# Turning the second layer's softmax weights on VectorE and through DRAM instead of on TensorE

## The chip, the cores and the metric

The kernel runs on one core of one Trainium2 chip. The metric is the device time of one execution in microseconds (us), taken as the median of several runs. Five engines matter here, each with its own queue that it works off strictly in order: TensorE (PE: matmuls, with its weight loads shown as PEld), VectorE (DVE), ScalarE (ACT), GpSimd (POOL, all but idle in this kernel) and SyncE (SP), which issues nearly all the transfers (DMAs). [...]

## The reference

Two decoder layers on a sequence of T = 512 tokens of width D = 2048, all in float32. The first layer is differential attention, the second "forgetting" attention over one shared set of keys and values. The change touches the second layer only. Cut to it, the reference is:

```
k, v, F = shared_kv(...)                       # F[t, head]: running sum of log forget gates
q, g = split(h @ w_q)                          # 16 heads of 128
for each block of 128 queries t, each head:
    sc = q[t] . k[s] / sqrt(128) + F[t] - F[s],   -1e30 where s > t
    p  = softmax(sc over s)
    o  = sum over s of p[t, s] * v[s]
y = (o * silu(g)) @ w_out
x = layer_norm(alpha * x + gate * y)
```

## The kernel before

**Products.** Every float32 operand X of a matmul is split into a rounded part hi (type fp32r) and the rest lo = X - hi. A product A x B is then three matmuls, hi x hi, hi x lo and lo x hi (`products`, lines 174 to 176). ScalarE makes hi (a copy that rounds), VectorE makes lo (a subtraction).

**The weight stream.** Weights come in "subs" of 256 rows by up to 512 columns: SP loads them (`wst`, four buffers), ScalarE copies them to `whi` (line 94), VectorE subtracts to `wlo` (line 95); `whi` and `wlo` have three buffers each. A `group` is one block of 512 output columns: 8 subs, and for each sub four "bursts" of six 512-wide matmuls, one burst for each PSUM bank (`acc`). So a group has 32 bursts and 192 `acc` matmuls. After its last burst each bank is read out (`evac`): for the second layer two banks become q (hi and lo) of two heads, two become their SiLU gates.

**Pieces between bursts.** After each burst `tick` takes one entry from a list, `pieces`, and runs it. In the second layer the pieces of a group are the attention of the pair of heads (a and b) whose q the group before made. So attention of pair p - 1 is laid into the matmuls of group p (`bj[p]`, eight groups), and the last pair into the first group of the output projection (`oB`), which starts right after.

**Attention of one head** (`attention_b`). A query block i of 128 has w = 128 (i + 1) keys. `score(i)`: three matmuls into `sc`, `biasb` from F and the mask (line 1208), sum and row minimum of the negated scores in one DVE instruction (line 1214), exponential with row sum on ScalarE (line 1217), reciprocal and scaling on VectorE (lines 1218, 1219). The result `eb` has queries on the partitions, but `values` needs keys on the partitions. `turn(i)` does that: i + 1 TensorE transposes of 128x128 into the PSUM tile `tr` (line 1228), ScalarE copies `tr` to `pTh` (line 1231), VectorE subtracts to `pTl` (line 1232). `values` then does twelve matmuls into `o` with `pTh` and `pTl` as moving operands, and line 1246 multiplies by the gate (`ogB`). There is one `pTh` and one `pTl`, so head b may write them only when head a's `values` have read them.

`attention_pair` fixes at which burst each step is handed over. The instructions are not run in that order: the framework plans every engine's queue anew from its own estimate of when each input is ready, and keeps that order on the chip. A few DVE instructions (line 1305, the first scaling of the residual, `nr`) are kept in the order in which they were written.

**The end of the layer.** In the first group of `oB` the last head's output must pass `ogB`, then `split_ogb` (`hh` on ScalarE, `hl` on VectorE), before the last k-tile of that same group can be multiplied. The same group also scales four residual tiles `nr` by two DVE instructions each (lines 1305 and 1306). `residual_b` puts these into entries of `pieces` that are None, from the third on, and the rest at the end of the list. When the group ends, line 926 (`ztmp`) empties each `acc` bank, and the next group waits for that.

Of the kernel before, what the change touches and what calls it, by code (L numbers as in the profile page):

```python
# [10 lines left out]
F32 = mybir.dt.float32  # L11
F32R = mybir.dt.float32r
I32 = mybir.dt.int32
AF = mybir.ActivationFunctionType
ALU = mybir.AluOpType

P = 128
D = 2048
KT = D // P
T = 512  # L20
TB = T // P
# [89 lines left out]
def tile_yoco(  # L111
# [23 lines left out]
    nc = tc.nc  # L135
    V, S, PE, G = nc.vector, nc.scalar, nc.tensor, nc.gpsimd
# [11 lines left out]
    dram = ctx.enter_context(tc.tile_pool(name="dram", bufs=1, space=bass.MemoryType.DRAM))  # L148
# [13 lines left out]
    def tr_bank(name="tr"):  # L162
        return ps.tile([P, 512], F32, name=name, tag="tr", bufs=1)
# [8 lines left out]
    def products(dst, lhs, rhs, start, stop):  # L172

        PE.matmul(dst, lhs[0], rhs[0], start=start, stop=False)  # L174
        PE.matmul(dst, lhs[0], rhs[1], start=False, stop=False)  # L175
        PE.matmul(dst, lhs[1], rhs[0], start=False, stop=stop)  # L176


    ident = const.tile([P, P], F32, name="ident")
# [3 lines left out]
    mask = const.tile([P, 512], F32, name="mask")  # L183
# [16 lines left out]
    pt = tr_bank()  # L200
# [7 lines left out]
    pt = tr_bank()  # L208
# [200 lines left out]
    def mod_rows(pool, fours, dst, bias, one):  # L409

        red = []

        def steps(n, acc):
            if n == 0:
                red.append(pool.tile([P, 64], F32, name="mred", tag="mred", bufs=2))
            t = pool.tile([P, 512], F32, name="mturn", tag="mturn", bufs=1)
            V.transpose(t, acc)
            V.tensor_reduce(  # L420
                red[0][:, 16 * n : 16 * n + 16], t.rearrange("p (j q) -> p j q", q=32), axis=mybir.AxisListType.X, op=ALU.add
            )
            if n == 3:
                row = pool.tile([64, 32], F32, name="mrow", tag="mrow", bufs=1)
                nc.sync.dma_start(row, bias.rearrange("(j q) -> j q", q=32))
            yield True
            if n == 3:
                pt = tr_bank()
                PE.matmul(pt[0:64, 0:32], red[0], fours, start=True, stop=True)
                V.scalar_tensor_tensor(row, pt[0:64, 0:32], one, row, op0=ALU.add, op1=ALU.add)  # L430
                nc.sync.dma_start(dst.rearrange("o (j q) -> (o j) q", q=32), row)
        return steps
# [5 lines left out]
    part = {}  # L438
    with tc.tile_pool(name="start", bufs=2, reuse_waits="tile") as sp, tc.manual_schedule(engines={ET.DVE}):
# [44 lines left out]
        def mod_steps():  # L484
            for n, (i, k, nr) in enumerate(tiles):
                k0, nk = sets[i]
                load_mods(n + NBUF)
                if k >= KT - on_pe(i):
                    continue
                if k == 0:  # L490
                    accs[i] = sp.tile([P, 2, 2 * P], F32, name="sacc", tag="sacc", bufs=2)
                acc = accs[i][:, :, : nk * P]
                for kq in range(nr):
                    w, sc = loaded[i, k][:, kq, :, :], cact[:, k + kq : k + kq + 1]
                    if k + kq == 0:
                        V.tensor_scalar(acc, w, sc, None, op0=ALU.mult)
                    else:
                        V.scalar_tensor_tensor(acc, w, sc, acc, op0=ALU.mult, op1=ALU.add)  # L498
                    yield i
# [3 lines left out]
        steps = mod_steps()  # L503
# [76 lines left out]
        todo = [(u, kt, kt == k0, kt == k1 - 1) for u, k0, k1 in phases for kt in range(k0, k1)]  # L580

        at = {"set": 0, "kt": 0, "go": 0}
        summed, turned = [], []
# [67 lines left out]
    for dst, src, col, bias, one in (  # L651
# [5 lines left out]
        steps = mod_rows(ap, fours, dst, bias[col : col + D], one)  # L657
# [358 lines left out]
    npool, n, nstats = zp  # L1016
# [83 lines left out]
    for i, (half, s) in enumerate(lag):  # L1100
# [7 lines left out]
        hi, lo = held[s]  # L1108
# [13 lines left out]
    for dst, col, one in ((mod_dram[1][1:2, :], D, 1.0), (gate_dram[1], 2 * D, 0.0)):  # L1122
        steps = mod_rows(npool, fours, dst, b_mod[1, col : col + D], one)
# [25 lines left out]

    bctx = ExitStack()  # L1150
    bp = bctx.enter_context(tc.tile_pool(name="bp", bufs=1, reuse_waits="tile"))
    pTh = bp.tile([P, TB, T], F32R, name="pTh")
    pTl = bp.tile([P, TB, T], F32R, name="pTl")

    V.tensor_scalar(pTh[:, 3, 256:384], mask[:, 0:P], 0.0, None, op0=ALU.mult)
    V.tensor_scalar(pTl[:, 3, 256:384], mask[:, 0:P], 0.0, None, op0=ALU.mult)
    ogB = [None] * B_HEADS

    def evac_b(p):
        def fn(b, acc):  # L1160
            hd = 2 * p + b % 2
            if b < 2:
                hi = bp.tile([P, T], F32R, name="qh", tag="qh", bufs=2)
                lo = bp.tile([P, T], F32R, name="ql", tag="ql", bufs=2)
                S.activation(hi, acc, AF.Copy, scale=QS)
                V.scalar_tensor_tensor(lo, acc, QS, hi.bitcast(F32), op0=ALU.mult, op1=ALU.subtract)
                cur[hd, "q"] = (hi, lo)
            else:
                th = bp.tile([P, T], F32, name="thb", tag="thb", bufs=1)
                sg = bp.tile([P, T], F32, name="sgb", tag="sgb", bufs=2)  # L1170
                S.activation(th, acc, AF.Tanh, scale=0.5)
                V.scalar_tensor_tensor(sg, th, 1.0, acc, op0=ALU.add, op1=ALU.mult)
                cur[hd, "sgT"] = sg
        return fn
# [21 lines left out]
    def attention_b(hd):  # L1196
        st = {}

        def score(i):
            def fn():  # L1200
                w = (i + 1) * P
                m = max(w, 256)
                q, k = cur[hd, "q"], cur[hd, "kB"]
                sc = sc_bank()
                ts = slice(i * P, (i + 1) * P)
                products(sc[:, :m], (q[0][:, ts], q[1][:, ts]), (k[0][:, :m], k[1][:, :m]), True, True)
                bias = bp.tile([P, 512], F32, name="biasb", tag="biasb", bufs=2)
                V.scalar_tensor_tensor(
                    bias[:, :w], cur[hd, "nf"][:, :w], F[:, i, hd : hd + 1], mask[:, (3 - i) * P :], op0=ALU.add, op1=ALU.add
                )  # L1210
                e = bp.tile([P, 512], F32, name="eb", tag="eb", bufs=3)
                mn = bp.tile([P, 1], F32, name="mnb", tag="mnb", bufs=3)
                rs = bp.tile([P, 1], F32, name="rsb", tag="rsb", bufs=3)
                V.tensor_tensor_reduce(  # L1214
                    out=e[:, :w], in0=sc[:, :w], in1=bias[:, :w], scale=-1.0, scalar=3.0e38, op0=ALU.add, op1=ALU.min, accum_out=mn
                )
                S.activation(e[:, :w], e[:, :w], AF.Exp, bias=mn, scale=-1.0, accum_out=rs)  # L1217
                V.reciprocal(rs, rs)
                V.tensor_scalar(e[:, :w], e[:, :w], rs, None, op0=ALU.mult)
                st["e", i] = e  # L1220
            return fn

        def turn(i):
            def fn():
                pt = tr_bank()
                e = st["e", i]
                for j in range(i + 1):
                    PE.transpose(pt[:, j * P : (j + 1) * P], e[:, j * P : (j + 1) * P], ident)  # L1228
                ts = slice(i * P, (i + 1) * P)
                src = pt[:, : (i + 1) * P].rearrange("p (j t) -> p j t", t=P)  # L1230
                S.copy(pTh[:, 0 : i + 1, ts], src)  # L1231
                V.tensor_tensor(pTl[:, 0 : i + 1, ts], src, pTh[:, 0 : i + 1, ts].bitcast(F32), op=ALU.subtract)  # L1232
            return fn

        def values(j0, j1):
            def fn():
                if j0 == 0:
                    st["o"] = o_bank()
                vh, vl = cur[hd // 2, "vB"]
                es = slice((hd % 2) * P, (hd % 2 + 1) * P)  # L1240
                for j in range(j0, j1):
                    t0 = min(j * P, 256)
                    products(st["o"][:, t0:], (vh[:, j, es], vl[:, j, es]), (pTh[:, j, t0:], pTl[:, j, t0:]), j == 0, j == 3)
                if j1 == TB:
                    ogB[hd] = ktile("ogB")
                    V.scalar_tensor_tensor(ogB[hd], st["o"], 0.5, cur[hd, "sgT"], op0=ALU.mult, op1=ALU.mult)
            return fn

        return [score(i) for i in range(TB)], [turn(i) for i in range(TB)], [values(0, 2), values(2, 4)]

    def attention_pair(p):
        sa, ta, va = attention_b(2 * p)
        sb, tb, vb = attention_b(2 * p + 1)
        return [
            None, None, sa[0], sa[1], ta[0], sa[2], ta[1], sa[3], ta[2], sb[0], ta[3], sb[1], va[0], sb[2], va[1], None, tb[0],
            tb[1], sb[3], tb[2], None, tb[3], None, vb[0], vb[1],
        ]

    def split_ogb(hds):
        for hd in hds:  # L1260
# [115 lines left out]
```

## Time and profile before

| | us |
|---|---|
| median of 3 runs (1995.78 to 1996.25) | 1996.07 |
| the profiled execution | 1992.9 |
| its span in the trace | 1991.1 |
| TensorE busy | 1955.8 (98%) |
| VectorE busy | 1320.8 (66%) |
| ScalarE busy | 708.2 (36%) |

The span runs from the first to the last instruction in the trace; the profiled execution has 1.8 us around it. Names in the profile are the program's tile names, `out<-in`; L1228 is line 1228 of the kernel. `DMA_DIRECT2D` is a transfer being issued by SP; "to landing" is the time from its issue until its data are there. The second layer's groups with attention lie from about 1420 us to 1850 us of the span, 54 us each.

### The profile page before, as it was taken

What the parts mean: (1) busy time and instruction counts of PE and PEld (TensorE: products, weight loads), DVE (VectorE), ACT (ScalarE), POOL (GpSimd) and SP (SyncE); (2) the same over time, 40 slices, a digit from 0 to 9 for tenths busy, and PEclk for the clock granted to TensorE, in tenths of its full rate; (3) what the DMA queues carried; (4) which work ended last, traced back from release to release, by engine and by line L of the source; (5) the groups of instructions that cost most, each with busy time, mean ns of one, the idle gap of its engine ahead of it and who ended that gap; (6) DMA issues with size and microseconds to landing.
All of it is one profiled execution on the core that took longest, in us unless ns stands there. A gap on an engine that the chain in (4) does not pass through costs nothing.

```text
span 1991.1 us, 24748 instructions
## 1 busy us (share of the span) xinstructions
PE 1955.8 (98%) x9079; PEld 1618.8 (81%) x9079; DVE 1320.8 (66%) x2404; ACT 708.2 (36%) x1217; POOL 2.2 (0%) x10
## 2 busy tenths in 40 slices
PE   5999999999999999999999999999999999999997
PEld 4888888888888888888888888888888888888886
DVE  7885667777777778853575656565555555576657
ACT  2432445333332334431273222224343434353123
POOL 0000000000000000000000000000000000000000
PEclk8999999999999999999999999999999999999999
DMA  9993444666667576552336676663333232232622
GB/s 344 348 317 96 143 149 157 191 213 201 211 191 227 186 232 203 189 170 98 127 128 227 233 239 199 223 212 127 96 96 100 96 105 92 96 120 96 232 92 106
DMA packets 259029, 343.81 MB, mean 173 GB/s; under 512 B 18614, under 2 KB 163404, under 8 KB 258140
## 3 DMA queue, kind: packets, MB, share of 16 engines
q1 hardware_dynamic: 256528, 338.02, 52.0%
q10 hardware_dynamic: 2380, 4.21, 0.6%
q8 instruction: 71, 1.16, 0.2%
q14 instruction: 50, 0.41, 0.1%
HBM read 329.51 MB, written 12.66 MB: 172 GB/s over the span
## 4 chain that ended last, share of the span: by engine, by line
PE 91%; DVE 4%; DMA 2%; issue 1%; ACT 1%; SPq 0%; DVEq 0%; ACTq 0%
PE acc L174 26%; PE acc L176 26%; PE acc L175 26%; PE sc L174 2%; PE sc L175 2%; PE sc L176 2%; PE o L176 1%; PE o L174 1%; PE o L175 1%; PE tr L1228 1%; DMA ms<-in_w_mod_dram 1%; DVE wlo L95 1%; DMA ms<-in_kv_w_mod_dram 1%; DVE sacc L498 1%; DVE macc L391 1%
## 5 line engine op out<-in xcount | busy, mean ns | idle before, releaser
L95 DVE TENSOR_TENSOR wlo<-wst,whi 128x1024 fp32r<-128x1024 f32 (+2 forms) x322 | 384.2, 1195 | 335.5 <-ACT whi L94 319.5
L94 ACT CAST whi<-wst 128x1024 fp32r<-128x1024 f32 (+2 forms) x322 | 331.8, 1031 | 662.2 <-PE acc L176 347.9
L174 PE MATMUL acc<-whi,hh 128*128 128x512 f32 x1232 | 484.3, 396 | 1.8 <-DVE sg L695 1.0
L175 PE MATMUL acc<-wlo,hh 128*128 128x512 f32 x1232 | 480.9, 390 | 0.1
L176 PE MATMUL acc<-whi,hl 128*128 128x512 f32 x1232 | 480.5, 390 | 0.0
L174 PE MATMUL acc<-hh,whi 128*128 128x512 f32 x1184 | 471.1, 398 | 0.6 <-DVE sg L695 0.6
L175 PE MATMUL acc<-hl,whi 128*128 128x512 f32 x1184 | 462.3, 390 | 0.0
L176 PE MATMUL acc<-hh,wlo 128*128 128x512 f32 x1184 | 461.7, 390 | 0.0
L174 PEld LDWEIGHTS acc<-whi,hh 128*128 128x128 f32 x1232 | 232.5, 189 | 48.5 <-DVE ztmp L926 1.2
L176 PEld LDWEIGHTS acc<-whi,hl 128*128 128x128 f32 x1232 | 231.3, 188 | 49.2
L175 PEld LDWEIGHTS acc<-wlo,hh 128*128 128x128 f32 x1232 | 231.6, 188 | 45.4 <-DVE wlo L95 0.5
L176 PEld LDWEIGHTS acc<-hh,wlo 128*128 128x128 f32 x1184 | 222.3, 188 | 48.8
L174 PEld LDWEIGHTS acc<-hh,whi 128*128 128x128 f32 x1184 | 222.6, 188 | 43.8 <-issue 1.9
L175 PEld LDWEIGHTS acc<-hl,whi 128*128 128x128 f32 x1184 | 222.8, 188 | 38.9
L391 DVE SCALAR_TENSOR_TENSOR macc<-ms,cact,macc 128x512 f32<-128x512 f32 x300 | 224.1, 747 | 37.6 <-DMA ms<-in_kv_w_mod_dram 21.8
L498 DVE SCALAR_TENSOR_TENSOR sacc<-sms,cact,sacc 128x512 f32<-128x512 f32 (+1 forms) x127 | 89.5, 704 | 5.0 <-DMA sms<-in_w_mod_dram 1.4
L725 ACT ACTIVATE e<-e,mn 128x128 f32<-128x128 f32 (+3 forms) x64 | 36.1, 564 | 120.6 <-DVE mn L721 120.5
L1217 ACT ACTIVATE eb<-eb,mnb 128x128 f32<-128x128 f32 (+1 forms) x64 | 36.0, 563 | 95.3 <-DVE mnb L1214 94.2
L1214 DVE CUSTOM_DVE_ANT_0 eb<-sc,biasb 128x128 f32<-128x128 f32 (+1 forms) x64 | 31.4, 490 | 55.3 <-PE sc L176 55.3
L1232 DVE TENSOR_TENSOR pTl<-tr,pTh 128x128 fp32r<-128x128 f32 (+1 forms) x64 | 31.1, 487 | 25.3 <-ACT pTh L1231 24.8
L391 DVE SCALAR_TENSOR_TENSOR macc<-msk,cact,macc 128x512 f32<-128x512 f32 x60 | 45.0, 749 | 1.4
L1231 ACT CAST pTh<-tr 128x128 fp32r<-128x128 f32 (+1 forms) x64 | 27.2, 424 | 44.3 <-PE tr L1228 43.5
(260 smaller groups left out, 1773.3 us busy)
## 6 DMA issues: line engine op xcount, KB each, us to landing
wst<-in_a_w_in_dram SPq DMA_DIRECT2D x240, 256.0 KB, 3.8
ms<-in_w_mod_dram SPq DMA_DIRECT2D x64, 512.0 KB, 4.4
ms<-in_kv_w_mod_dram SPq DMA_DIRECT2D x64, 512.0 KB, 4.2
wst<-in_kv_w_dram SPq DMA_DIRECT2D x64, 512.0 KB, 3.9
wst<-in_b_w_in_dram SPq DMA_DIRECT2D x128, 256.0 KB, 2.9
sms<-in_w_mod_dram SPq DMA_DIRECT2D x56, 512.0 KB, 6.9
wst<-in_a_w_out_dram SPq DMA_DIRECT2D x32, 512.0 KB, 3.7
msk<-in_w_mod_dram SPq DMA_DIRECT2D x64, 256.0 KB, 5.5
```

The lines of the kernel that those rows point to most:

```text
L94: self.nc.scalar.copy(hi[:, :, :w], st[:, :, :w])
L95: self.nc.vector.tensor_tensor(lo[:, :, :w], st[:, :, :w], hi[:, :, :w].bitcast(F32), op=ALU.subtract)
L174: PE.matmul(dst, lhs[0], rhs[0], start=start, stop=False)
L175: PE.matmul(dst, lhs[0], rhs[1], start=False, stop=False)
L176: PE.matmul(dst, lhs[1], rhs[0], start=False, stop=stop)
L391: ins = V.scalar_tensor_tensor(acc, w, cact[:, kt : kt + 1], acc, op0=ALU.mult, op1=ALU.add)
L498: V.scalar_tensor_tensor(acc, w, sc, acc, op0=ALU.mult, op1=ALU.add)
L725: S.activation(e[:, :w], e[:, :w], AF.Exp, bias=mn, scale=-1.0, accum_out=rs)
L1214: V.tensor_tensor_reduce(out=e[:, :w], in0=sc[:, :w], in1=bias[:, :w], scale=-1.0, scalar=3.0e38, op0=ALU.add, op1=ALU.min, accum_out=mn)
L1217: S.activation(e[:, :w], e[:, :w], AF.Exp, bias=mn, scale=-1.0, accum_out=rs)
L1231: S.copy(pTh[:, 0 : i + 1, ts], src)
L1232: V.tensor_tensor(pTl[:, 0 : i + 1, ts], src, pTh[:, 0 : i + 1, ts].bitcast(F32), op=ALU.subtract)
```

## The change

`turn` no longer uses TensorE. VectorE's transpose instruction turns each 32x32 block in place (`tb`), SP writes the result to a DRAM tile (`turned`), and four DMAs per query block (`send`), one for each group of 32 partitions, read it back in the order that makes a full transpose, into `pTl`. `take` then copies `pTl` to `pTh` on ScalarE and replaces `pTl` by the difference on VectorE. `pTh` and `pTl` have a new layout: [key, query / 32, key block, query % 32], so that one DMA row writes (i + 1) x 128 contiguous bytes; the moving operand of `values` thereby becomes runs of 32 elements with a step of 128 elements. `eb` now has one buffer for each query block, `thb` shares the two buffers of `biasb`. For each pair of heads 20 transposes leave TensorE; 8 block transposes come to VectorE, and 8 writes and 32 reads to SP. The list of steps of a pair has 26 entries instead of 25, and its only empty ones are the first two (before: also entries 15, 20 and 22).

```diff
-    pTh = bp.tile([P, TB, T], F32R, name="pTh")
-    pTl = bp.tile([P, TB, T], F32R, name="pTl")
...
+    pTh = bp.tile([P, 16, TB, 32], F32R, name="pTh")
+    pTl = bp.tile([P, 16, TB, 32], F32R, name="pTl")
...
-                th = bp.tile([P, T], F32, name="thb", tag="thb", bufs=1)
+                th = bp.tile([P, T], F32, name="thb", tag="biasb", bufs=2)
...
-                e = bp.tile([P, 512], F32, name="eb", tag="eb", bufs=3)
+                e = bp.tile([P, w], F32, name="eb", tag=f"eb{i}", bufs=1)
...
         def turn(i):
             def fn():
-                pt = tr_bank()
-                e = st["e", i]
-                for j in range(i + 1):
-                    PE.transpose(pt[:, j * P : (j + 1) * P], e[:, j * P : (j + 1) * P], ident)
-                ts = slice(i * P, (i + 1) * P)
-                src = pt[:, : (i + 1) * P].rearrange("p (j t) -> p j t", t=P)
-                S.copy(pTh[:, 0 : i + 1, ts], src)
-                V.tensor_tensor(pTl[:, 0 : i + 1, ts], src, pTh[:, 0 : i + 1, ts].bitcast(F32), op=ALU.subtract)
+                t = bp.tile([P, (i + 1) * P], F32, name="tb", tag=f"tb{i}", bufs=1)
+                V.transpose(t.rearrange("p (b j c) -> p j b c", b=4, c=32), st["e", i].rearrange("p (j b c) -> p j b c", b=4, c=32))
+                st["t", i] = dram.tile([P, (i + 1) * P], F32, name="turned", tag=f"turned{i}", bufs=2)
+                nc.sync.dma_start(st["t", i], t)
+            return fn
+
+        def send(i):
+            def fn():
+                src = st["t", i].rearrange("(a r) (b n) -> b r a n", a=4, b=4)
+                to = pTl[:, 4 * i : 4 * i + 4, 0 : i + 1, :].bitcast(F32).rearrange("p a j c -> p a (j c)")
+                for b in range(4):
+                    nc.sync.dma_start(to[32 * b : 32 * b + 32], src[b])
+            return fn
+
+        def take(i):
+            def fn():
+                hi, lo = (t[:, 4 * i : 4 * i + 4, 0 : i + 1, :] for t in (pTh, pTl))
+                S.copy(hi, lo.bitcast(F32))
+                V.tensor_tensor(lo, lo.bitcast(F32), hi.bitcast(F32), op=ALU.subtract)
             return fn
...
-                    products(st["o"][:, t0:], (vh[:, j, es], vl[:, j, es]), (pTh[:, j, t0:], pTl[:, j, t0:]), j == 0, j == 3)
+                    m0 = t0 // 32
+                    o = st["o"][:, t0:].rearrange("p (m c) -> p m c", c=32)
+                    products(o, (vh[:, j, es], vl[:, j, es]), (pTh[:, m0:, j, :], pTl[:, m0:, j, :]), j == 0, j == 3)
...
     def attention_pair(p):
-        sa, ta, va = attention_b(2 * p)
-        sb, tb, vb = attention_b(2 * p + 1)
-        return [
-            None, None, sa[0], sa[1], ta[0], sa[2], ta[1], sa[3], ta[2], sb[0], ta[3], sb[1], va[0], sb[2], va[1], None, tb[0],
-            tb[1], sb[3], tb[2], None, tb[3], None, vb[0], vb[1],
+        sa, ra, da, ta, va = attention_b(2 * p)
+        sb, rb, db, tb, vb = attention_b(2 * p + 1)
+        steps = [
+            [], [], [sa[0]], [sa[1]], [ra[0]], [sa[2], ra[1]], [da[0]], [sa[3], da[1]], [ra[2]], [sb[0], ta[0]],
+            [ra[3], da[2]], [sb[1], ta[1]], [rb[0], da[3]], [sb[2], ta[2]], [rb[1]], [sb[3], ta[3]],
+            [va[0], rb[2]], [va[1]], [db[0], db[1], rb[3]], [db[2]], [tb[0], db[3]], [tb[1]], [tb[2]], [tb[3]], [vb[0]], [vb[1]],
         ]
+        return [(lambda todo=todo: [fn() for fn in todo]) if todo else None for todo in steps]
```

More of the change, by code (lines that the diff above doesn't have):

```diff
@@ L1151, in tile_yoco @@
     bp = bctx.enter_context(tc.tile_pool(name="bp", bufs=1, reuse_waits="tile"))
-    pTh = bp.tile([P, TB, T], F32R, name="pTh")
-    pTl = bp.tile([P, TB, T], F32R, name="pTl")
-    V.tensor_scalar(pTh[:, 3, 256:384], mask[:, 0:P], 0.0, None, op0=ALU.mult)
-    V.tensor_scalar(pTl[:, 3, 256:384], mask[:, 0:P], 0.0, None, op0=ALU.mult)
+    pTh = bp.tile([P, 16, TB, 32], F32R, name="pTh")
+    pTl = bp.tile([P, 16, TB, 32], F32R, name="pTl")
+    for t in (pTh, pTl):
+        V.tensor_scalar(t[:, 8:12, 3, :], mask[:, 0:P].rearrange("p (m c) -> p m c", c=32), 0.0, None, op0=ALU.mult)
     ogB = [None] * B_HEADS
@@ L1247, in values @@
             return fn
-        return [score(i) for i in range(TB)], [turn(i) for i in range(TB)], [values(0, 2), values(2, 4)]
+        parts = (score, turn, send, take)
+        return *([part(i) for i in range(TB)] for part in parts), [values(0, 2), values(2, 4)]
     def attention_pair(p):
-        sa, ta, va = attention_b(2 * p)
-        sb, tb, vb = attention_b(2 * p + 1)
-        return [
-            None, None, sa[0], sa[1], ta[0], sa[2], ta[1], sa[3], ta[2], sb[0], ta[3], sb[1], va[0], sb[2], va[1], None, tb[0],
-            tb[1], sb[3], tb[2], None, tb[3], None, vb[0], vb[1],
+        sa, ra, da, ta, va = attention_b(2 * p)
[4 more added lines that the diff above has]
+            [va[0], rb[2]], [va[1]], [db[0], db[1], rb[3]], [db[2]], [tb[0], db[3]], [tb[1]], [tb[2]], [tb[3]], [vb[0]], [vb[1]],
         ]
+        return [(lambda todo=todo: [fn() for fn in todo]) if todo else None for todo in steps]
     def split_ogb(hds):
```

## The prediction

> **What bounds the kernel now.** I read the page's totals first, then busy time by stretch, the chain that ended last inside one stretch, and last the rows around one transpose.
>
> ```profile
> span 1991.1 us, 24748 instructions
> PE 1955.8 (98%) x9079; PEld 1618.8 (81%) x9079; DVE 1320.8 (66%) x2404; ACT 708.2 (36%) x1217; POOL 2.2 (0%) x10
> ...
> PE 91%; DVE 4%; DMA 2%; issue 1%; ACT 1%; SPq 0%; DVEq 0%; ACTq 0%
> ```
>
> ```profile
> 1420.00:1474.00 54.00, 54.00 (x262) 45.02 (x261) 31.25 (x66) 21.31 (x40) 0.00 (x0) 1.00 0.31 99
> 1474.00:1528.00 54.00, 54.00 (x262) 45.03 (x261) 31.25 (x66) 21.31 (x40) 0.00 (x0) 1.00 0.31 98
> ...
> 1744.00:1798.00 54.00, 54.00 (x262) 45.12 (x261) 39.45 (x80) 28.33 (x54) 0.00 (x0) 1.00 0.39 121
> 1798.00:1852.00 54.00, 53.22 (x256) 43.84 (x255) 38.33 (x77) 17.86 (x34) 0.00 (x0) 1.00 0.40 139
> ```
>
> The columns are busy us of PE, PEld, DVE, ACT and POOL, then granted clock, DMA share and GB/s. In a pair's 54 us TensorE never idles at full clock; DVE has 23 us to spare, ACT 33, the DMA engines two thirds. Only work taken from TensorE's queue shortens this stretch, and any new TensorE wait lengthens it by its full size.
>
> **What leaves TensorE.** The chain within that stretch, and the rows around three transposes:
>
> ```profile
> by line: PE acc L175 27.5%; PE acc L174 27.4%; PE acc L176 27.1%; PE tr L1228 4.2%; PE sc L175 2.4%; PE sc L176 2.4%; PE o L175 2.4%; PE o L176 2.4%; PE sc L174 2.4%; PE o L174 2.3%
> ```
>
> ```profile
> L1228 PE MATMUL tr<-ident,eb x160: 270/272/328, 1422.5 to 1831.3; 128*128 128x128 f32 x160
> ```
>
> ```profile
> 1429.16 0.39 PE L175 MATMUL acc<-hl,whi 128*128 128x512 f32 x1
> 1429.39 0.39 PE L176 MATMUL acc<-hh,wlo 128*128 128x512 f32 x1
> 1429.62 0.49 PE L1228 MATMUL tr<-ident,eb 128*128 128x128 f32 x3
> 1429.87 0.49 PE L174 MATMUL acc<-hh,whi 128*128 128x512 f32 x1
> 1430.19 0.39 PE L175 MATMUL acc<-hl,whi 128*128 128x512 f32 x1
> ```
>
> Matmuls overlap, so a transpose's 272 ns is not its price. An `acc` matmul starts every 0.23 us (1429.16, 1429.39). From 1429.39 to the second `acc` start after the transposes (1430.19) are 0.80 us where 0.46 would do: 0.34 for three, 0.113 each. The chain agrees: 4.2% of 54 us is 2.27 us for 20. All 160: **-18.0 us**.
>
> [...]
>
> **What DVE and ACT get.** The nearest rows are a block transpose of another stage, and the groups of this one:
>
> ```profile
> L419 DVE STREAM_TRANSPOSE mturn<-macc x24: 700/710/714, 286.7 to 1341.9; 128x512 f32<-128x512 f32 x24
> ```
>
> ```profile
> L95 DVE TENSOR_TENSOR wlo<-wst,whi 128x1024 fp32r<-128x1024 f32 x72 | 88.1, 1224 | 79.9 <-ACT whi L94 78.7
> L1232 DVE TENSOR_TENSOR pTl<-tr,pTh 128x512 fp32r<-128x512 f32 x16 | 11.1, 691 | 16.0 <-ACT pTh L1231 15.9
> L1214 DVE CUSTOM_DVE_ANT_0 eb<-sc,biasb 128x512 f32<-128x512 f32 x16 | 11.1, 691 | 18.3 <-PE sc L176 18.3
> L170 DVE TENSOR_TENSOR kbl<-kT,kbh 128x512 fp32r<-128x512 f32 x16 | 10.9, 687 | 0.0
> L1219 DVE TENSOR_SCALAR eb<-eb,rsb 128x512 f32<-128x512 f32 x16 | 7.7, 484 | 0.2
> ```
>
> ```profile
> L1217 ACT ACTIVATION_READ_ACCUMULATOR eb<-eb,mnb 128x1 f32 x64 | 12.0, 187 | 0.0
> L1217 ACT ACTIVATE eb<-eb,mnb 128x512 f32<-128x512 f32 x16 | 11.6, 723 | 3.6 <-DVE mnb L1214 2.5
> L169 ACT CAST kbh<-kT 128x512 fp32r<-128x512 f32 x16 | 9.8, 619 | 11.5 <-PE sc L176 11.5
> L1165 ACT ACTIVATE qh<-acc 128x512 fp32r<-128x512 f32 x16 | 9.6, 599 | 9.6 <-PE acc L176 9.6
> L1231 ACT CAST pTh<-tr 128x512 fp32r<-128x512 f32 x16 | 9.4, 587 | 22.8 <-PE tr L1228 22.8
> ```
>
> By size a head's four block transposes cost about 0.28 + 0.42 + 0.56 + 0.71 = 2.0 us, 4 a pair, inside DVE's 23 spare. The copies and subtractions of `take` replace those of `turn` one for one. None of it is on the path unless `values` waits for it, so the queues must be walked.
>
> **Pair clock**, 0 at a group's first burst, from the built program's order: TensorE runs scores after 18, 24, 36, 48 (head a), 60, 72, 84, 96 (head b) `acc` matmuls; head a's `values` start after 112, their second matmul (the first to read `pTl`) after 115; head b's after 187 and 190 of 192. With 0.23 us each, 3.8 for the pair's scores and 1.9 for a head's `values` this is 29.6 and 30.5, and 48.7 and 49.6. The group ends at 51.7.
>
> *Head a.* The last score of head b is in PSUM 1.1 us after the 96th `acc`. Then ACT does `kbh`, the exponential (0.72 + 0.19) and the copy of a's block 3, ready 3.3 us after that `acc`; needed 4.6 after. DVE does 0.70 (reduce), 1.14 (`wlo`), 0.1, 0.60 (`kbl`), 0.48, 0.7 (block transpose), 0.7 (subtraction): 5.6 after; needed 5.5 after. I take a wait of 0.1 us, 8 times: **+0.8** (ends 0 and 0.5 each, so 0 to 4).
>
> *Head b.* Its copy for block 3 stands behind the second `qh`: 0.42 + 0.60 + 0.59 = 1.6 us after bank 1's last matmul, and its subtraction ends at 2.45; needed at 1.8 and 2.7. No wait: 0 (up to 0.3 each, 2).
>
> **The DMAs.** SP's rows:
>
> ```profile
> L47 SPq DMA_DIRECT2D wst<-in_b_w_in_dram x128: 367/422/572, 1340.7 to 1747.7; - x128
> ```
>
> ```profile
> wst<-in_b_w_in_dram SPq DMA_DIRECT2D x16, 256.0 KB, 2.9
> ```
>
> ```profile
> gate_dram<-mrow SPq DMA_DIRECT2D x1, 8.0 KB, 1.7
> ```
>
> ```profile
> mod_dram<-mrow SPq DMA_DIRECT2D x1, 8.0 KB, 3.2
> ```
>
> ```profile
> 1342.00:1352.00 10.00, 10.00 (x46) 8.02 (x45) 7.50 (x13) 4.39 (x6) 0.00 (x0) 1.00 0.33 104
> 1218.00:1228.00 10.00, 10.00 (x46) 8.01 (x45) 6.62 (x9) 1.86 (x2) 0.00 (x0) 1.00 0.62 186
> ```
>
> A pair now has 16 + 3 + 40 = 59 issues; at 0.42 us SP is busy 25 of 51.7 us. The 40 move 2.6 MB in 5120 pieces of 128 to 2048 bytes, beside 5.3 MB in about 4900 pieces: a DMA share of 0.46 (by bytes) to 0.65 (by pieces). A small transfer landed after 1.7 us at a share of 0.33, after 3.2 at 0.62; I take 2.5, and 2.9 for block 3's 256 KB.
>
> Head a, block 3: score 12.9, reduced 14.0, exponential done 15.4 (ACT first does `whi`, `kbh` and a's block 0), scaled and turned on DVE 17.5, written by 20.4, read back by four issues from 20.7 to 22.4 (they wait behind the write of b's block 0), landed 24.5. ACT's copy has its turn at 28: spare 3.5 us. Head b: `pTl` is free from 30.5 to 32.2; 16 reads of 0.42 end at 39, the last landing at 41.5; its copy is behind `qh` at 47.9: spare 6. The weight loads that now stand behind these waits lose up to 8 us; each `wst` is loaded four subs ahead and its `whi` made two subs ahead, 6.5 us a sub, so they stay hidden. Sum for the DMAs: 0.
>
> **The last pair.** It lies in the output projection's first group, where the planned order differs: ACT makes the `whi` of the sub after next before it copies b's blocks 2 and 3, and DVE puts three `nr` scalings ahead of b's last subtraction and three behind it (in the old order two pairs of them ran before the last subtraction).
>
> ```profile
> 1834.45 1.05 ACT L94 CAST whi<-wst 128x1024 fp32r<-128x1024 f32 x1 [2.16 <-PE acc L176]
> ```
>
> ```profile
> 1839.70 0.69 DVE L1305 SCALAR_TENSOR_TENSOR nr<-nr,g 128x512 f32<-128x512 f32 x1
> 1840.42 0.69 DVE L1306 SCALAR_TENSOR_TENSOR nr<-b,nr 128x512 f32<-128x512 f32 x1
> ...
> 1845.39 0.68 DVE L1306 SCALAR_TENSOR_TENSOR nr<-b,nr 128x512 f32<-128x512 f32 x1
> 1845.99 0.68 DVE L1305 SCALAR_TENSOR_TENSOR nr<-nr,g 128x512 f32<-128x512 f32 x1
> ```
>
> ```profile
> 1850.93 0.50 PE L174 MATMUL acc<-whi,hh 128*128 128x512 f32 x1 [0.78 <-DVE ztmp L926]
> ```
>
> Independent 512-wide DVE instructions follow at 0.60 us, dependent ones at 0.72. Count from the start x of the last matmul of sub 6, which frees that `whi`. `whi` x+0.45 to 1.5, `wlo` to 2.7, b's block 2 to 3.2, three `nr` to 5.1, b's block 3 to 5.8. TensorE has only the 12 matmuls of k-tile 14 to fill and wants block 3 at x+3.2: waits **2.6**. Its `values` end at 7.6; DVE's three further `nr` end at 7.7, `ogB` 8.4, `hh` 9.1, and k-tile 15 waits **1.6**. DVE is then `hl`, `nr` and the first two bank reads until 12.3, and has 12 instructions (7.2 us) ahead of the third bank's `ztmp`, done at 20.2; TensorE wants that bank 26 matmuls into the next group, at 17.8: waits **2.4**. Together 6.6, where before there was the one wait of 0.78: **+5.8** (2 if half is covered, 10 if residual tiles come late too).
>
> **Sum.** -18.0 + 0.8 + 0 + 0 + 5.8 = -11.4. The profiled execution took 1992.9, the median of runs is 3.2 above it: 1981.5 for a profile, 1996.1 - 11.4 = **1985 us** for the median.
>
> **Rivals.**
> 1. *The way through DRAM is late (slower).* Place: ACT's copy of a's block 3, on which `values` of head a wait. Block 0 has two landings before it, and block 0's copy stands ahead of the exponential of block 3, which has two more: 1 us more for each landing costs about 4 us at the end, less 1 of slack. The 3.5 us are gone at landings about 1.1 us longer than taken, near 3.6; past that each 0.1 us costs 0.4 us in each of 8 pairs. At 4.0 the gain is gone; at 4.5 the time is 1985 + 29 = 2014. For it: 3.2 us in the busier stretch. Against it: 2.9 for 256 KB in this one. Chance 0.16. [...]
> 2. *Small waits at `values`.* The planner puts TensorE's `values` where it expects their inputs, so an error of its estimates of 0.5 us at both places would cost 16 x 0.5 = 8 us: 1993; of 0.8 us, 1998. For it: I find almost no slack at head a. Against it: no TensorE idling in any of the seven stretches from 1420 to 1798 us now. Chance 0.2.
> 3. *Moving operands in runs of 32 elements are read more slowly.* No row shows such a read. If `values` doubled, 3.8 us a pair, 30 in all: 2015. Chance 0.06.
> 4. *Nothing is gained*, the transposes being hidden now: the chain lists them with 2.27 us per stretch, so 0.02.
>
> **Chances.** The forecast with its bounds (0.56) is 1977 (-18 and a little) to 1992; rival 2 gives faster in most of its 0.2. About 0.2%, 4 us, is what a measurement of this kernel can tell from no change. Faster 0.73, same 0.05, slower 0.22. The range for 8 in 10 runs from 1977, where all 18 us arrive with half the end's waits, to 2003, inside rival 1.
>
> **What would show it.** Right: the pair's stretch 51.7 to 52.2 us with TensorE busy throughout; no L1228 on TensorE; small transfers landing below 3.4 us; TensorE waits in front of `pTl` and `hh` once, in the last pair, of 2 to 3 and 1 to 2 us, then one for `ztmp`. Wrong: TensorE waiting for `pTh` or `pTl` in every pair (rivals 1 and 2, told apart by whether ACT's copy waits for a DMA), `o` matmuls starting further apart than 0.23 us for 512 columns (rival 3), or `whi` waiting for `wst`.

## The result, and the profile after

The changed kernel takes 1984.79 us (median of 6 runs, 1981.44 to 1985.82); the kernel before, run beside it, 1996.11 (6 runs, 1995.78 to 1997.05). The ratio is 0.9941, with a 95% interval of 0.9928 to 0.9953. On a second chip it was 1982.59 against 1994.39, again 0.9940 (0.9928 to 0.9953). The forecast was 1985 against 1996.1. The profiled execution took 1985.8 us.

The head of the page of the changed kernel:

```profile
span 1984.0 us, 25164 instructions
PE 1941.0 (98%) x8919; PEld 1606.7 (81%) x8919; DVE 1345.7 (68%) x2468; ACT 704.4 (36%) x1217; POOL 2.2 (0%) x10
...
PE 90%; DVE 5%; DMA 3%; issue 1%; SPq 1%; ACT 1%; DVEq 0%; ACTq 0%
```

There are 160 matmuls fewer (9079 to 8919) and 64 DVE instructions more (2404 to 2468); TensorE is still what bounds the kernel. Busy times by stretch, columns as in the prediction (PE, PEld, DVE, ACT, POOL, granted clock, DMA share, GB/s):

```profile
1474.00:1526.00 52.00, 52.00 (x243) 43.40 (x242) 34.57 (x76) 20.78 (x40) 0.00 (x0) 1.00 0.52 153
1734.00:1786.00 52.00, 52.00 (x243) 43.43 (x242) 42.04 (x89) 27.97 (x53) 0.00 (x0) 1.00 0.60 178
1786.00:1838.00 52.00, 48.07 (x216) 39.93 (x215) 34.46 (x71) 16.27 (x32) 0.00 (x0) 0.97 0.58 177
1838.00:1850.00 12.00, 9.69 (x36) 7.53 (x35) 11.05 (x18) 0.55 (x1) 0.00 (x0) 0.86 0.58 225
```

TensorE is busy throughout the pairs. Only the last pair has gaps, and there the granted clock falls below 1 (0.97 and 0.86 in the last two rows). The length of a pair is read from ScalarE's `qh`, which comes twice in each group, at the same point of its matmuls; the first of the two, in the kernel before and in the changed one, five groups apart:

```profile
1465.08 0.60 ACT L1165 ACTIVATE qh<-acc 128x512 fp32r<-128x512 f32 x1 [0.49 <-PE acc L176]
...
1735.14 0.60 ACT L1165 ACTIVATE qh<-acc 128x512 fp32r<-128x512 f32 x1 [0.49 <-PE acc L176]
```

```profile
1463.31 0.60 ACT L1166 ACTIVATE qh<-acc 128x512 fp32r<-128x512 f32 x1 [0.53 <-PE acc L176]
...
1721.65 0.60 ACT L1166 ACTIVATE qh<-acc 128x512 fp32r<-128x512 f32 x1 [0.53 <-PE acc L176]
```

270.06 / 5 = 54.01 us became 258.34 / 5 = 51.67: **2.34 us a pair**. All that TensorE waits for from 1365 us to the end of the last pair (line, releaser, us in total, times, longest):

```profile
PE o L175 <- DVE pTl L1246: 2.5, 1, 2.5
PE acc L174 <- DVE ztmp L926: 2.3, 1, 2.3
PE acc L174 <- ACT hh L169: 1.4, 1, 1.4
```

These are the three waits of the forecast, each once: 2.6, 2.4 and 1.6 were foretold.

**Where the 7.1 us between the two profiled spans come from.** Eight pairs at 2.34 us are 18.7. The three waits, 6.2 us in place of 0.78, give 5.4 back. Half clock behind two of them (last section) gives back 3.0. Of the 3.2 us that are left, 2.7 were there before the change begins: the first `qh` of the second layer comes at 1413.79 us instead of 1411.10, after waits in the first layer that differ from execution to execution. (In a second profile of the changed kernel, with a span of 1979.2 us, it comes at 1412.04; of the 4.8 us between the two spans 1.8 are there, and the other 3.0 are the half clock, which the second does not have.) The profiled execution of before was 3.2 us faster than its own median, as the prediction said, so this part is not the change's.

### The profile page after: what moved, and what is told of

It reads as the page before. It is cut to its first block, busy times and chain, and to the rows that moved or that the text cites. A ratio compares the mean times of both kernels' runs of the same rounds, so it can differ in the third digit from the quotient of the medians.

```text
span 1984.0 us, 25164 instructions
## 1 busy us (share of the span) xinstructions
PE 1941.0 (98%) x8919; PEld 1606.7 (81%) x8919; DVE 1345.7 (68%) x2468; ACT 704.4 (36%) x1217; POOL 2.2 (0%) x10
## 4 chain that ended last, share of the span: by engine, by line
PE 90%; DVE 5%; DMA 3%; issue 1%; SPq 1%; ACT 1%; DVEq 0%; ACTq 0%
PE acc L174 26%; PE acc L175 26%; PE acc L176 26%; PE sc L174 2%; PE sc L175 2%; PE sc L176 2%; PE o L174 1%; PE o L175 1%; PE o L176 1%; DMA ms<-in_w_mod_dram 1%; DVE macc L391 1%; DMA ms<-in_kv_w_mod_dram 1%; DVE wlo L95 1%; SPq L471 0%; PE tr L742 0%
## 5 line engine op out<-in xcount | busy, mean ns | idle before, releaser
L174 PE MATMUL acc<-hh,whi 128*128 128x512 f32 x1184 | 465.5, 393 | 1.0 <-DVE sg L695 1.0
L721 DVE CUSTOM_DVE_ANT_0 e<-sc,bias 128x128 f32<-128x128 f32 (+3 forms) x64 | 31.0, 485 | 15.2 <-PE sc L176 15.1
L791 ACT ACTIVATE ogT<-tr,subg 128x128 f32<-128x128 f32 x64 | 20.0, 363 | 46.1 <-PE tr L789 46.0
```

The costliest lines, as they stand in the source:

```text
L721: V.tensor_tensor_reduce(out=e[:, :w], in0=sc[:, :w], in1=st["bias"][:, (3 - i) * P :], scale=-1.0, scalar=3.0e38, op0=ALU.add, op1=ALU.mi ...
L791: S.activation(ogT[2 * h + e][:, i * P : (i + 1) * P], pt[:, e * P : (e + 1) * P], AF.Copy, scale=subg[:, e : e + 1])
```

## Experiments

All were timed beside the kernel before on the same chip; ratios are against it. None leaves a part of the computation out.

### The transposes put back on TensorE, unread

```diff
                 nc.sync.dma_start(st["t", i], t)
+                pt = tr_bank()
+                for j in range(i + 1):
+                    PE.transpose(pt[:, j * P : (j + 1) * P], st["e", i][:, j * P : (j + 1) * P], ident)
             return fn
```

> The changed kernel, with the 160 TensorE transposes put back into turn beside the new way; they write the PSUM tile tr, which nothing reads, so the output is the same and only TensorE's share of the removed work is added. My theory (TensorE is full, every matmul start costs): 160 x 0.113 = +18 us on the changed kernel, 2003 us. Rival (the transposes were hidden beside other work and the gain came from elsewhere): 1985 to 1988 us. By the full duration of one (272 ns) it would be +44, 2029 us.

Measured: 2002.61 us against 1994.64, ratio 1.0041 (1.0027 to 1.0055), as the theory had it. With the transposes back, the rest of the change makes the kernel slower than the kernel before, so the gain comes from the time that TensorE is spared. A stretch by busy time, in this experiment:

```profile
1474.00:1528.00 54.00, 54.00 (x261) 44.79 (x260) 34.19 (x73) 20.80 (x39) 0.00 (x0) 1.00 0.49 147
```

The first `qh` of the same two groups come at 1465.13 and 1735.85 us: 54.14 a pair, 2.47 more than without the transposes. Eight pairs make 19.8 us, and the ratios (1.0041 against 0.9941) differ by 1.00%, which is 20 us: 0.124 us for each transpose, against 0.117 by the change itself and 0.113 by the start-to-start rows of the prediction. That 20 and 19.8 agree so closely is in part luck: TensorE's waits in the last pair are 4.4 us here (`hh` 1.4, `ztmp` 2.4 and 0.6; none for `pTl`) in place of 6.2, and the interval of each ratio is some 5 us wide.

### The last pair as it was before

```diff
+    def on_pe(hd):
+        return hd >= 14
...
     def attention_pair(p):
+        if p == 7:
+            return [
+                None, None, sa[0], sa[1], ra[0], sa[2], ra[1], sa[3], ra[2], sb[0], ra[3], sb[1], va[0], sb[2], va[1], None, rb[0],
+                rb[1], sb[3], rb[2], None, rb[3], None, vb[0], vb[1],
+            ]
```

> The last pair of heads alone goes back to TensorE transposes and to the old list of steps; the other seven pairs keep the way through DRAM. My theory: the three TensorE waits of the last pair (2.5 + 1.4 + 2.3 us) and the two stretches at half clock behind them (1.4 + 1.6 us) go, one wait of 0.8 and 20 transposes (2.3 us) come: 1984.8 - 9.2 + 3.1 = 1979 us. Rival (the end's time is set by VectorE's residual work, whatever turns the weights): waits stay, 1987 us.

`on_pe` names the last two heads; their `turn` is the old one, writing the new layout. Measured: 1979.77 us against 1994.64, ratio 0.9927 (0.9914 to 0.9939). Of the three waits one is left, with the 0.8 us that it had in the kernel before, and the clock is 1.00 to the end of the group:

```profile
PE acc L174 <- DVE ztmp L926: 0.8, 1, 0.8
```

So the waits come from the last pair's form alone, as the theory had it. The time does not show as much: by the ratios this version is 2.8 us faster than the change, where the theory, which started from an execution with half clock, had 6, and the intervals of 0.9927 and 0.9941 overlap. Its gain rests on its waits and on the combined version below.

### The residual scalings earlier in the last pair

```diff
         if f == 0:
             free = [k for k, piece in enumerate(pieces) if piece is None and k > 1]
-            for k, b in zip(free, banks):
-                pieces[k] = lambda b=b: scaled(b)
-            pieces.extend(lambda b=b: scaled(b) for b in banks[len(free):])
+            for k, b in zip((18, 19, 20, 21), banks):
+                pieces[k] = lambda b=b, step=pieces[k]: (step(), scaled(b))
```

> The changed kernel, with the four residual scalings of the first output group handed over at entries 18 to 21 of the last pair's list instead of at its end; nothing else. My theory: VectorE has no nr ahead of the last subtraction, so the waits become 0.7 + 1.6 + 1.2 = 3.5 us instead of 6.2, and with no wait above 2 us the clock stays full (another 3.0 us): 1979 us. Rival A (the transfers of the last head are what is late): the first wait stays at 2.5, 1985 us. Rival B (the clock falls whatever the length of the wait): 1982 us.

Measured: 1980.89 us against 1994.64, ratio 0.9928 (0.9915 to 0.994). The waits:

```profile
PE acc L174 <- DVE ztmp L926: 2.3, 1, 2.3
PE acc L174 <- ACT hh L169: 1.4, 1, 1.4
PE o L175 <- DVE pTl L1246: 0.6, 1, 0.6
```

Moving the `nr` pairs out from ahead of b's last subtraction takes the first wait from 2.5 to 0.6 us, which shows its cause and refutes rival A. The clock stayed at 1.00 behind all three waits in this profile, against rival B; but it did so behind one of 2.3 us, so the run does not bear out the theory's limit of 2 us either; that limit was an estimate, between the waits of 1.4 us without and 2.3 us with half clock behind them in the first profile of the changed kernel. `ztmp` was expected to shrink to 1.2 and stayed at 2.3. VectorE reaches the first two bank reads some 3 us earlier than in the changed kernel, but then stands until the next group's first residual tile has come from DRAM, and has that group's scalings to do before it reads the third bank:

```profile
1834.25 0.69 DVE L1324 SCALAR_TENSOR_TENSOR nr<-nr,g 128x512 f32<-128x512 f32 x1 [1.07 <-DMA nr<-n_dram]
```

The 1.07 us are as much as the expectation fell short by, 1.1; that they are the whole reason was not tested apart.

### The kernel before, with its residual scalings at the end

```diff
-            free = [k for k, piece in enumerate(pieces) if piece is None and k > 1]
+            free = []
```

> The kernel before, with its four residual scalings at the end of the list, as the new list's lack of empty entries has them; transposes stay on TensorE. My theory: the bank reads come some 3 us later on VectorE, of which up to 2.4 us reach TensorE: 1996 to 1999 us, with no wait in front of pTl or hh. Rival (the list alone makes the end's loss): three waits as in the changed kernel, 2002 to 2005 us.

Measured: 1995.83 us against 1994.64, ratio 1.0006 (0.9997 to 1.0015). TensorE waits 2.2 us for `ztmp` in all (before: 0.8), and never for `pTl` or `hh`:

```profile
PE acc L174 <- DVE ztmp L926: 2.2, 2, 1.6
```

The loss of the list's empty entries alone costs the old kernel 1.4 us of waits; in the time, 1.2 us by the ratio, it does not stand clear of nothing (none to 3). The waits for `pTl` and `hh` need the longer way of the new `turn` as well.

### One more trip through DRAM for each block

```diff
-                nc.sync.dma_start(st["t", i], t)
+                first = dram.tile([P, (i + 1) * P], F32, name="passed", tag=f"passed{i}", bufs=2)
+                nc.sync.dma_start(first, t)
+                nc.sync.dma_start(st["t", i], first)
```

> Every block of the changed kernel makes one more trip: from DRAM to a second DRAM tile (passed) and only then to pTl. The planner reacts by itself and puts head a's values 9 acc matmuls (2 us) later and head b's just behind the start of the next group. Theory (a landing took 2.0 us where the walk took 2.5, so the way through DRAM has some 5 us to spare at head a, and one more trip costs two of them, about 5 us, against those 5 us plus the 2 us of delay): TensorE waits for pTh or pTl in none of the first seven pairs; 1985, 1983 to 1988. Rival (the way through DRAM is nearly on the path, so that landings of the length taken would have been late): two trips of 2.0 to 2.5 us show up as a wait of 1.5 to 3 us at head a in each of 8 pairs, 1995 to 2010.

Measured: 1993.4 us against 1994.39, ratio 0.9995 (0.9987 to 1.0004): nearly the whole gain is gone, but in the way of neither theory. TensorE is still full in the seven pairs (the first row of the busy times below, with a DMA share of 0.59 in place of 0.52). The loss stands in the last pair: a wait of 8.2 us in place of 2.5, and half clock behind it and behind a later wait of 1.9 us (last rows):

```profile
1474.00:1526.00 52.00, 52.00 (x240) 43.26 (x239) 35.14 (x82) 20.91 (x42) 0.00 (x0) 1.00 0.59 177
...
1834.00:1838.00 4.00, 2.73 (x7) 2.10 (x8) 0.69 (x1) 0.62 (x1) 0.00 (x0) 0.50 1.03 374
...
1854.00:1858.00 4.00, 4.00 (x12) 3.15 (x11) 3.23 (x5) 0.18 (x1) 0.00 (x0) 0.57 0.00 0
```

```profile
PE o L174 <- ACT pTh L1247: 8.2, 1, 8.2
```

SyncE's queue and ScalarE's copies there:

```profile
1814.69 0.89 SPq L1232 DMA_DIRECT2D passed<-tb  x2
1821.16 0.80 SPq L1241 DMA_DIRECT2D pTl<-turned  x2
1822.05 0.47 SPq L1233 DMA_DIRECT2D turned<-passed  x1
1822.57 2.94 SPq L1241 DMA_DIRECT2D pTl<-turned  x6
1825.56 0.47 SPq L1233 DMA_DIRECT2D turned<-passed  x1
...
1828.74 1.77 SPq L1241 DMA_DIRECT2D pTl<-turned  x4
```

```profile
1829.75 0.51 ACT L1247 CAST pTh<-pTl 128x384 fp32r<-128x384 f32 x1 [2.27 <-DMA pTl<-turned]
1834.60 0.62 ACT L1247 CAST pTh<-pTl 128x512 fp32r<-128x512 f32 x1 [4.34 <-DMA pTl<-turned]
```

The planner put head a's `values` of the last pair at 1820.49 us here; in the changed kernel they start at 1809.44. SyncE stood from 1815.6 to 1821.2 us in front of the first reads for head b, which may write `pTl` only when head a has read it. In the changed kernel these sixteen reads begin at 1810.56 and take 7.44 us; here they begin 10.6 us later, and behind the first of them in the queue stood the second trips of b's last two blocks, whose first trips had been issued by 1815.6. Block 3's second trip went out at 1825.6, its reads from 1828.7, and ScalarE could copy at 1834.6. Without the two trips among them the reads would have ended at 1828.6 instead of 1830.5, an estimate from the 7.44 us; so most of the delay comes from the late `values` of head a, and some 2 us from the order in SyncE's queue. Block 3's reads then also landed late, after a median of 4.6 us beside large weight loads (DMA share 1.01 from 1830 to 1834 us).

The theory's outcome held for the seven pairs and failed for the last. Its reason is not shown: the planner put head a's `values` not 2 us later, as the expectation had it, but 3.9 us in the first pair and 5 to 10 in the others (by the start of their second matmul, counted from the group's `qh`), as much as the 5 us that the expectation put on one more trip, or more. So the run does not tell whether the changed kernel has room for one, and it leaves the rival untested in these pairs. What it shows is that the longer way cost TensorE nothing in the seven pairs, where the readers were put later (busy 52.00 of 52.00 us in the row above), and that in the last pair, where the next stage needs the head at once, it reached TensorE (8.2 us).

### Only the last head by TensorE, and the residual scalings earlier

```diff
+    def on_pe(hd):
+        return hd == 15
...
-            for k, b in zip(free, banks):
-                pieces[k] = lambda b=b: scaled(b)
-            pieces.extend(lambda b=b: scaled(b) for b in banks[len(free):])
+            for k, b in zip((14, 18, 20, 22), banks):
+                pieces[k] = lambda b=b, step=pieces[k]: (step and step(), scaled(b))
```

The last pair's list is written anew for it, with head b's `turn` steps at entries 18, 19, 21 and 23 and its `values` at the end.

> Only the very last head is turned on TensorE (10 transposes, 1.1 us), and the four first residual scalings are handed over at entries 14, 18, 20 and 22 of the last pair's list. Theory (the three waits of the last pair come from where its last steps stand in the queues, and everything else of the change is gain): -18.0 + 1.1 for head 15, waits of about 1 us for ztmp alone as in the kernel before: 1978, 1976.5 to 1979.5, and full clock to the end of the group. Rival (the waits come back elsewhere, since the residual scalings only change places on VectorE): 1980 to 1983.

Measured: 1977.06 us against 1994.39, ratio 0.9914 (0.9901 to 0.9928), where the changed kernel on the same chip had 0.9940 (its five runs 1981.02 to 1983.56, these four 1975.53 to 1979.31). Clock 1.00 in the last pair and behind it, and one wait, as the theory had it:

```profile
PE acc L174 <- DVE ztmp L926: 0.6, 1, 0.6
```

This version beats both kernels: 10 of the 160 transposes, 1.1 us, and the earlier scalings together buy back nearly all that the last pair had lost. What each does alone in this form was not run.

### Matmuls in place of the idling, and the changed kernel once more

In the first of the two, 20 unread 512-wide matmuls are handed over in the last pair:

```diff
+            if layer == 1 and k == 1:
+                fill = tr_bank()
+                for _ in range(20):
+                    PE.matmul(fill, Hh[0][:, 0:P], Hh[0], start=True, stop=True)
```

> The changed kernel with 20 unread 512-wide matmuls in the last pair, which the planner lays into the places where TensorE waits: 11 around the pTl wait (2.5 us), 7 ahead of the last k-tile (1.4 us); they cost nothing where TensorE would wait. Theory (the half clock behind the first wait is brought on by the idling itself): the o matmuls of the last head start 0.23 us apart all through, 1.4 us less than the changed kernel: 1983.5, or up to 1.5 less if the ztmp wait also loses its half clock. Rival (the drop of the clock has nothing to do with the idling): o matmuls 0.43 apart again, 1985 to 1986.

> The changed kernel on the chip of these three: 1985, waits of 2.5, 1.4 and 2.3 us in the last pair; half clock behind some of them in some executions: a spread of 3 us or more between executions.

Measured against 1994.39: 1981.82 us with the extra matmuls (ratio 0.9933, 0.992 to 0.9947), 1982.59 without (0.994, 0.9928 to 0.9953; the spread of its five runs is 2.5 us, a little under the 3 foretold). The waits for `pTl` and `hh` are gone with them and that for `ztmp` is down to 1.6 us, and no matmul starts at half clock. But the 20 matmuls take 20 x 0.23 = 4.6 us, and the waits lost are 6.2 - 1.6 = 4.6, so nothing is left to see; and the changed kernel itself shows no half clock in this second profile, with the same waits. The experiment does not tell its two theories apart.

## Why the prediction was right

- **What leaves TensorE: -18.0.** Right in kind, a little low: 2.34 us a pair instead of 2.27, 18.7 in all, and 2.47 a pair, 19.8 in all, without the small waits of the next point, as the transposes put back show. With TensorE full, what counted here was the marginal time of a transpose, 0.113 to 0.124 us, and not the 0.272 us of its row.
- **The `values`: +0.8 at head a, 0 at head b.** About right in sum, wrong in place. The walk's terms for head a add up to 5.5 us, when the data are needed, not to its 5.6. No wait of TensorE shows in the list, but its weight loads wait in the seven pairs, for `pTh` as well as for `pTl`:

```profile
PEld o L174 <- ACT pTh L1245: 1.6, 6, 0.3
PEld o L175 <- DVE pTl L1246: 1.5, 7, 0.4
```

```profile
1465.83 0.50 PE L174 MATMUL o<-pTh,vbh 128*128 128x512 f32 x1
1466.16 0.40 PE L174 MATMUL acc<-hh,whi 128*128 128x512 f32 x1
```

  Most of it is hidden behind the matmul before. What is left can be read from the starts: 0.33 us instead of 0.23 behind head b's first matmul (above), 0.26 behind head a's first on `pTl` (rows further down), and so within 0.01 in the first six pairs. That is 0.13 us a pair, an estimate of 1.0 in all, most of it at head b, which was put at 0; and it matches the difference between 2.47 and 2.34.
- **VectorE's new work.** Right: block transposes of 512 columns take 0.71 us as in the row of the other stage, and DVE goes from 31.25 of 54 us to 34.57 of 52.
- **The DMAs: 0.** Right, and with more room than walked. The transfers in one pair's stretch (KB each, median us to landing):

```profile
wst<-in_b_w_in_dram SPq DMA_DIRECT2D x16, 256.0 KB, 2.9
turned<-tb SPq DMA_DIRECT2D x2, 256.0 KB, 2.0
pTl<-turned SPq DMA_DIRECT2D x8, 64.0 KB, 2.5
...
pTl<-turned SPq DMA_DIRECT2D x8, 16.0 KB, 2.0
```

  Landings of 1.8 to 2.5 (medians by size) where 2.5 to 2.9 were taken, at a share of 0.52, inside the 0.46 to 0.65. The list of waits from 1420 to 1790 us has none of `whi` for `wst`.
- **The last pair: +5.8.** Right in place, order and size: 2.6, 1.6 and 2.4 us foretold, 2.5, 1.4 and 2.3 measured; 5.4 more than before. What the step left out is the clock behind the waits, up to 3 us more.
- **Sum.** -11.4 foretold, -11.3 and -11.8 measured on two chips. That it comes so close is in part luck: -19.8 + 1.0 + 5.4 = -13.4 by the traces, 2 us more gain than foretold, against the half clock, which takes back up to 3 us in some executions and was not in the sum.

The rivals. *The way through DRAM* did not come about: reads and writes landed alike (median 2.0 us, the slowest 4.4 and 3.7), where the rival set in near 3.6. The extra trip shows that data that come late by this way hold TensorE up, 8.2 us at the last pair's head b; at head a, where the rival had it, that run does not test it. *Small waits at `values`*: there, but 0.13 us a pair and not 0.5 at both places. *Runs of 32 elements*: refuted, as head a's matmuls follow each other in the changed kernel at the pace of contiguous ones, 0.23 us for 512 columns, and 0.26 only behind the first that reads `pTl`, whose weight load had waited:

```profile
1447.98 0.42 PE L175 MATMUL o<-pTl,vbh 128*128 128x512 f32 x1
1448.24 0.40 PE L176 MATMUL o<-pTh,vbl 128*128 128x512 f32 x1
1448.47 0.34 PE L174 MATMUL o<-pTh,vbh 128*128 128x384 f32 x1
```

*Nothing is gained*: refuted by the transposes put back, +20 us.

## What to carry to other kernels

Where one engine is full, price what is taken from it by start-to-start distances, not by the duration of one instruction, and let the replacement be as long-winded as the others' idle time allows: the block transposes, writes, reads and copies of a pair cost TensorE some 0.13 us of its 52 here. Then look at the one place without a next group to hide behind: the last turn of the loop lost 5.4 of 18.7 us, and giving its last head the short way back, with the residual scalings moved forward, won 5.5 us of median time (1982.59 to 1977.06). Where a planner sets the order, look at what it did before reading a result: with the extra trip it moved the readers by more than the trip. And in that run reads that waited for a buffer held up the writes behind them in the same queue, some 2 us of the 8.2 by the estimate above.

## What was not expected of the hardware

After waits of 1.9 us and more TensorE ran at half clock for a while in five cases of eight, counted below. In the first profile of the changed kernel, the rows behind the wait of 2.50 us and, later, behind that of 2.31:

```profile
1829.05 0.63 PE L175 MATMUL o<-pTl,vbh 128*128 128x512 f32 x1 [2.50 <-DVE pTl L1246]
1829.48 0.63 PE L176 MATMUL o<-pTh,vbl 128*128 128x512 f32 x1
...
1846.61 0.63 PE L174 MATMUL acc<-whi,hh 128*128 128x512 f32 x1
1847.04 0.63 PE L175 MATMUL acc<-wlo,hh 128*128 128x512 f32 x1
...
1849.60 0.46 PE L175 MATMUL acc<-wlo,hh 128*128 128x512 f32 x1
1849.90 0.39 PE L176 MATMUL acc<-whi,hl 128*128 128x512 f32 x1
```

Starts are 0.43 us apart instead of 0.23, and the second stretch begins 1.3 us after the end of its wait and lasts some 3.4 us. In the second profile the same two waits, to the hundredth, are followed by full speed:

```profile
1827.30 0.50 PE L175 MATMUL o<-pTl,vbh 128*128 128x512 f32 x1 [2.50 <-DVE pTl L1246]
1827.64 0.40 PE L176 MATMUL o<-pTh,vbl 128*128 128x512 f32 x1
...
1841.95 0.50 PE L174 MATMUL acc<-whi,hh 128*128 128x512 f32 x1 [2.31 <-DVE ztmp L926]
1842.28 0.39 PE L175 MATMUL acc<-wlo,hh 128*128 128x512 f32 x1
```

Over all profiles of these kernels, from the second layer's first group on and as far as the waits were read (to 1870 us or later), half clock followed five of the eight waits of 1.9 us or more, all in the last pair or in the group behind it (2.5 and 2.3 in the first profile, 2.4 with the transposes back, 8.2 and 1.9 with the extra trip; not 2.5 and 2.3 in the second profile, not 2.3 with the residual early), and none of the waits of 1.6 us or less that began at full clock. The two ends of the kernel are left out of this count: in the kernel before the clock is 0.68 from 30 to 40 us, 0.83 from 40 to 50 and 0.50 over the last 9, in the first profile of the changed kernel 0.66, 0.83 and 0.56, and nothing was changed there.

The shortest wait with half clock behind it was 1.9 us (with the extra trip: 0.57 granted from 1854 to 1858 us), and the same 2.5 and 2.3 us were followed by half clock in one execution and not in the next. What makes one wait fall on one side or the other stays open: no run here shows it.
